# Stick-breaking attention ranked in front of the ten projection blocks of a hybrid mixer

## The chip, the core and the metric

The kernel runs on one core of a Trainium2 chip. The metric is the device time of one execution in microseconds, as the median of three runs. The profile is one further execution, recorded by the hardware profiler. Engines are named as the profile names them: PE is TensorE's matmul, PEld its weight load, DVE VectorE, ACT ScalarE, POOL GpSimd, SP the engine that issues most loads.

## The reference, cut to what matters

One transformer block on 512 tokens of width 1024, all in float32. The first half normalises the input, projects it, runs four mixers on the projections, gates and sums them:

```python
xn = _rms_norm(h, norm_mix_g)
(cb, cc, cx, uv, sb_q, sb_k, sb_v, fx_q, fx_k, fx_v, f_raw, gate_raw) = split(xn @ w_in)
y_a = _short_conv_mixer(cb, cc, cx, w_conv)                   # cb * conv3(cc * cx)
y_b = _spatial_gating_mixer(uv, w_s, b_s, ln_g, ln_b)         # gelu, layer norm of v, causal mix
y_c = _stick_breaking_attention(sb_q, sb_k, sb_v)             # 4 heads of 64
y_d = _forgetting_attention(rms(fx_q), rms(fx_k), fx_v, cumsum(log_sigmoid(f_raw + b_f)))
merged = sum_n sigmoid(gate_raw[n]) * (y_n @ w_branch[n])
h = h + merged @ w_out
h = h + _swiglu(_rms_norm(h, norm_ffn_g), w_ffn_in, w_ffn_out)
```

The change lies in the first half: the projections of `cc`, `cx`, `cb`, `fx_q`, `fx_k`, the gating mixer and the stick-breaking attention.

## The kernel before

Activations are kept transposed, 128 channels by 512 tokens to a tile. Every float32 product is made of three fp32r products of a high and a low part (`mm3`, L185 to L198): high by high, high by low, low by high. The weights' parts are made on the chip: `load_units` (L207) loads a chunk of 128x1024 on SP's queue into `raw`, then `split` (L179) copies it to `whi` on ACT (L180) and subtracts on DVE to get `wlo` (L181). `raw`, `whi` and `wlo` have three buffers each, and a tile's name carries a number that counts up in the order of the code (`whi_535` is the high part of the last chunk of the first token group).

The stretch around the change, in the order of the code:

- `u` blocks, then the first token group `wt1` (L377, four chunks, four PSUM banks of the pool "a", L196 to L198), which gives the gating mixer's v and the stick-breaking v; then gelu, layer norm and split of v into `vg` (L405 to L424), and the causal weights `wsh`, `wsl` (L428 to L434, with a load on ACT's queue and a select on POOL).
- `mixed(MIXED[:8])`, eight of the ten projection blocks. A block (`proj_block`) is 8 units of weights, that is one chunk, 24 matmuls of 512 columns into one of three PSUM banks "g". `conv_block` (L463) is for the convolution, `fox_block` (L441) for the forgetting q and k; the latter's norm is `fox_norm` (L451), two matmuls, a square root on ACT, a reciprocal on DVE.
- the gating mixer's 24 matmuls (L505 to L507), which read `vg`, in four banks "a" of the five.
- the second token group `wt2` (two chunks of 128x1040, four banks "a"), which gives the forgetting v and f.
- the four heads of the stick-breaking attention: `sb_scores` (L548, matmuls L567 to L569, absolute value on ACT L571), `sb_weights` (exp, log, splits, matmuls L600 to L609, exp), `values` (L530, L535). A head holds four banks "a" from its scores to its weights.
- `mixed(MIXED[8:])`, the last two blocks, then the forgetting attention, then four passes of gates: a gate block of 24 matmuls and a branch of 6 for each of eight d.

Within an engine the instructions are not issued in the order of the code. A scheduler takes the code's order as rank and, engine by engine, puts in the instruction of the lowest rank whose operands are ready on a timeline that it estimates; the result is one fixed order for each engine. So PE runs projection blocks and gates while a head of attention is on ACT and DVE. Each engine then runs its list in order, and an instruction that waits holds up all that stand behind it.

Of the kernel before, what the change touches and what calls it, by code (L numbers as in the profile page):

```python
# [51 lines left out]
MIXED = (("cc", 0), ("cx", 0), ("fxq", 0), ("cb", 0), ("fxk", 0), ("cc", 1), ("fxq", 1), ("cx", 1), ("fxk", 1), ("cb", 1))  # L52
# [75 lines left out]
def mixer_kernel(ctx, tc, xT, units, quads, wt1, wt2, wsT, small, out):  # L128
# [312 lines left out]
    def fox_block(n, b):  # L441
        t = slot("y")
        V.tensor_tensor(t, proj_block(OFF[n] + b * P), r1, op=ALU.mult)
        fx[n, b] = t
        sq = slot("tmp")
        S.activation(sq, t, AF.Square)
        sqh, sql = slot("tmp", F32R), slot("tmp", F32R)
        split(sqh, sql, sq)
        return n, t, sq, sqh, sql

    def fox_norm(n, t, sq, sqh, sql):  # L451
        ps = bank("g")
        PE.matmul(out=ps, lhsT=hm_r, rhs=sqh, start=True, stop=False)
        PE.matmul(out=ps, lhsT=hm_r, rhs=sql, start=False, stop=True)
        S.activation(sq, ps, AF.Sqrt, bias=eps)
        V.reciprocal(sq, sq)
        g = gq if n == "fxq" else sml[:, C_GK:C_GK + 1]
        V.scalar_tensor_tensor(t, t, g, sq, op0=ALU.mult, op1=ALU.mult)
# [4 lines left out]
    def conv_block(n, b):  # L463
        ps = proj_block(OFF[n] + b * P)
        if n == "cc":
            cv[b] = slot("gt")
            V.tensor_tensor(cv[b], ps, r1, op=ALU.mult)
        elif n == "cx":
            cx, acc = slot("gt"), slot("gt")
            V.tensor_tensor(cx, ps, r1, op=ALU.mult)  # L470
            V.tensor_tensor(cx, cv[b], cx, op=ALU.mult)
            w = [sml[:, C_CONV + 3 * b + i:C_CONV + 3 * b + i + 1] for i in range(3)]
            V.tensor_scalar(acc, cx, w[2], None, op0=ALU.mult)
            V.scalar_tensor_tensor(acc[:, 1:], cx[:, :T - 1], w[1], acc[:, 1:], op0=ALU.mult, op1=ALU.add)
            V.scalar_tensor_tensor(acc[:, 2:], cx[:, :T - 2], w[0], acc[:, 2:], op0=ALU.mult, op1=ALU.add)
            V.tensor_tensor(acc, acc, r1, op=ALU.mult)
            cv[b] = acc
        else:
            V.tensor_tensor(cv[b], ps, cv[b], op=ALU.mult)
            split(*y[0, b], cv[b])  # L480

    def mixed(blocks):
        norm = None
        for n, b in blocks:
            if n in ("fxq", "fxk"):
                norm = fox_block(n, b)
            else:
                conv_block(n, b)
                if norm:
                    fox_norm(*norm)  # L490
                norm = None

    mixed(MIXED[:8])


    for b in range(2):
        for c2 in range(2):
# [125 lines left out]
            scores = sb_scores(h + 1)  # L623
        values(h, sbv, *weights, [y[2, 0], y[2, 1]], js)

    mixed(MIXED[8:])


    before = sm.tile([P, NT, HEADS], F32, tag="before", bufs=1, name="before")
# [405 lines left out]
```

## Time and profile before

| what | us |
|---|---|
| median of 3 runs (792.93 to 793.89) | 793.47 |
| the profiled execution, whole | 792.95 |
| its span, first to last instruction | 791.2 |
| PE busy in the span | 785.9 |
| DVE busy | 546.5 |
| ACT busy | 367.8 |

The profiled execution takes 1.75 us more than its span. A matmul's busy time reaches past the start of the next one, since matmuls are pipelined; so PE's work is counted here from start to start, and a short wait shows as a longer step between two starts.

### The profile page before, as it was taken

The page shows a single profiled execution, that of the slowest core. Times are in us where ns is not written, and L with a number is a line of the kernel's source. Part 1 is how long each engine was busy: PE and PEld are TensorE (multiplying, and loading weights), DVE is VectorE, ACT ScalarE, POOL GpSimd, SP SyncE. Part 2 cuts the span into 40 slices and gives each one's busy share as a digit, 9 for nine tenths or more (in the row PEclk, how much of TensorE's full clock was granted, in tenths as well). Part 3 has the DMA queues.
Part 4 walks back from the last instruction along what each step waited for, and adds up shares of the span by engine and source line. Part 5 has one row for each costly group of instructions (what it writes and reads, how often), then busy time and mean ns, then how long its engine had stood idle before and what let it go on. Part 6 is the DMA issues. An engine that isn't in the chain of part 4 may idle for free.

```text
span 791.2 us, 10770 instructions
## 1 busy us (share of the span) xinstructions
PE 785.9 (99%) x4319; PEld 677.7 (86%) x4319; DVE 546.5 (69%) x780; ACT 367.8 (46%) x522; POOL 8.4 (1%) x23
## 2 busy tenths in 40 slices
PE   9999999999999999999999999999999999999998
PEld 6888888888888888888888888998899998899987
DVE  8447886877677688756665698873478874468752
ACT  7336427677743455434343554552155552135530
POOL 1000000000000000000000000000000000000000
PEclk9999999999999999999999999999999999999999
DMA  7423222222123222222243343352133333211021
GB/s 286 133 80 104 97 80 81 80 81 74 59 80 106 81 81 81 80 93 81 106 161 119 131 155 115 108 184 82 54 107 109 107 119 121 80 54 54 28 94 67
DMA packets 24098, 78.98 MB, mean 100 GB/s; under 512 B 2672, under 2 KB 2928, under 8 KB 24048
## 3 DMA queue, kind: packets, MB, share of 16 engines
q1 hardware_dynamic: 22608, 75.80, 28.4%
q10 hardware_dynamic: 1440, 2.49, 1.0%
q8 instruction: 34, 0.56, 0.3%
q14 instruction: 16, 0.13, 0.1%
HBM read 76.18 MB, written 2.10 MB: 99 GB/s over the span
## 4 chain that ended last, share of the span: by engine, by line
PE 97%; ACT 1%; DVE 0%; DMA 0%; issue 0%; SPq 0%
PE ps L187 65%; PE ps L891 8%; PE ps L892 8%; PE ps L890 7%; PE ps L198 1%; PE ps L196 1%; PE ps L197 1%; PE ps L535 1%; PE ps L701 1%; DMA raw<-units 0%; PE ps L685 0%; PE ps L601 0%; PE ps L568 0%; PE ps L600 0%; PE ps L686 0%; PE ps L569 0%
## 5 line engine op out<-in xcount | busy, mean ns | idle before, releaser
L187 PE MATMUL ps<-xg,whi 128*128 128x512 f32 (+1 forms) x1212 | 377.8, 393 | 0.5 <-DVE xg L181 0.3
L187 PEld LDWEIGHTS ps<-xg,whi 128*128 128x128 f32 x1212 | 226.2, 188 | 50.3 <-DVE xg L181 0.8
L187 PE MATMUL ps<-xg,wlo 128*128 128x512 f32 (+1 forms) x606 | 235.8, 393 | 0.0
L180 ACT ACTIVATE whi<-raw 128x1024 fp32r<-128x1024 f32 (+2 forms) x104 | 106.4, 1025 | 180.1 <-PE ps L187 135.7
L181 DVE TENSOR_TENSOR wlo<-raw,whi 128x1024 fp32r<-128x1024 f32 (+2 forms) x104 | 122.8, 1182 | 49.7 <-ACT whi L180 49.4
L891 PE MATMUL ps<-op,whi 128*128 128x256 f32 x504 | 141.0, 281 | 0.0
L890 PE MATMUL ps<-op,whi 128*128 128x256 f32 x504 | 140.6, 280 | 0.0
L892 PE MATMUL ps<-op,wlo 128*128 128x256 f32 x504 | 139.2, 281 | 0.0
L187 PEld LDWEIGHTS ps<-xg,wlo 128*128 128x128 f32 x606 | 113.9, 188 | 24.9
L180 ACT ACTIVATE whi<-sraw 128x1024 fp32r<-128x1024 f32 x63 | 66.9, 1062 | 97.3 <-PE ps L187 32.7
L890 PEld LDWEIGHTS ps<-op,whi 128*128 128x128 f32 x504 | 95.3, 189 | 0.2
L891 PEld LDWEIGHTS ps<-op,whi 128*128 128x128 f32 x504 | 94.7, 188 | 0.2
L892 PEld LDWEIGHTS ps<-op,wlo 128*128 128x128 f32 x504 | 93.9, 188 | 0.0
L181 DVE TENSOR_TENSOR wlo<-sraw,whi 128x1024 fp32r<-128x1024 f32 x63 | 77.1, 1224 | 23.1 <-ACT whi L180 22.9
L187 PE MATMUL ps<-y,whi 128*128 128x512 f32 x224 | 70.5, 394 | 0.0
L962 DVE TENSOR_TENSOR mrg<-ps,mrg 128x512 f32<-128x512 f32 (+1 forms) x25 | 16.7, 669 | 64.5 <-PE ps L187 64.5
L187 PEld LDWEIGHTS ps<-y,whi 128*128 128x128 f32 x224 | 42.0, 188 | 9.7
L187 PE MATMUL ps<-y,wlo 128*128 128x512 f32 x112 | 44.2, 394 | 0.0
L727 ACT ACTIVATE gt<-gt 128x512 f32<-128x512 f32 x32 | 20.1, 627 | 23.7 <-DVE gt L726 23.4
L726 DVE TENSOR_TENSOR gt<-ps,r 128x512 f32<-128x512 f32 x32 | 22.0, 687 | 11.3 <-PE ps L187 11.2
L187 PEld LDWEIGHTS ps<-y,wlo 128*128 128x128 f32 x112 | 21.0, 188 | 4.8
L737 DVE SCALAR_TENSOR_TENSOR gt<-gt,ps 128x512 f32<-128x512 f32 x24 | 16.4, 685 | 10.1 <-PE ps L187 6.7
(247 smaller groups left out, 827.7 us busy)
## 6 DMA issues: line engine op xcount, KB each, us to landing
raw<-units SPq DMA_DIRECT2D x90, 512.0 KB, 3.4
sraw<-quads SPq DMA_DIRECT2D x36, 512.0 KB, 4.5
x<-xT SPq DMA_DIRECT2D x8, 256.5 KB, 5.2
raw<-units SPq DMA_DIRECT2D x8, 256.0 KB, 5.2
raw<-wt SPq DMA_DIRECT2D x4, 512.0 KB, 3.9
tmp<-xT ACTq DMA_DIRECT2D x8, 256.0 KB, 3.6
outT<-mrg SPq DMA_DIRECT2D x7, 256.0 KB, 2.0
raw<-wt SPq DMA_DIRECT2D x2, 520.0 KB, 3.3
```

What stands on the lines that cost most here:

```text
L180: S.activation(dst_hi, src, AF.Copy)
L181: V.tensor_tensor(dst_lo, src, f(dst_hi), op=ALU.subtract)
L187: i = PE.matmul(**args)
L196: PE.matmul(out=ps, lhsT=ah, rhs=bh, start=start, stop=False)
L197: PE.matmul(out=ps, lhsT=al, rhs=bh, start=False, stop=False)
L726: V.tensor_tensor(t, proj_block(OFF["gate"] + n * D + d * P), r1, op=ALU.mult)
L727: S.activation(t, t, AF.Tanh, scale=0.5)
L737: V.scalar_tensor_tensor(t, t, 1.0, ps, op0=ALU.add, op1=ALU.mult)
L890: PE.matmul(out=dst, lhsT=wh[:, u], rhs=xh[:, k], start=first and k == 0 and jj == 0, stop=False, skip_group_check=True)
L891: PE.matmul(out=dst, lhsT=wh[:, u], rhs=xl[:, k], start=False, stop=False, skip_group_check=True)
L892: PE.matmul(out=dst, lhsT=wl[:, u], rhs=xh[:, k], start=False, stop=ends, skip_group_check=True)
L962: V.tensor_tensor(h1[d][:, cs], src, h1[d][:, cs], op=ALU.add)
```

## The change

The call of the first eight blocks is taken out of its place ahead of the gating mixer, and all ten blocks are called behind the stick-breaking attention. The order of the units in the weight stream is the same. Both programs have 4301 matmuls; the changed one has 20 loads of an activation table on ACT, the one before 16.

```diff
@@ -490,8 +490,6 @@
                     fox_norm(*norm)
                 norm = None
 
-    mixed(MIXED[:8])
-
 
     for b in range(2):
         for c2 in range(2):
@@ -623,7 +621,7 @@
             scores = sb_scores(h + 1)
         values(h, sbv, *weights, [y[2, 0], y[2, 1]], js)
 
-    mixed(MIXED[8:])
+    mixed(MIXED)
```

Line numbers behind L492 are two lower in the changed kernel (L505 becomes L503). The code now asks for the two chunks of `wt2` ahead of the first projection block, and for the attention's banks ahead of the blocks' work. Three places of the engines' lists follow.

PE at the end of the first token group. Before (`ps_628` and `ps_661` are the blocks cc 0 and cx 0):

```order
L187 MATMUL ps_628<-xg_310,whi_630 128x512 x2
L187 MATMUL ps_628<-xg_310,wlo_631 128x512
L187 MATMUL ps_661<-xg_139,whi_663 128x512 x2
L187 MATMUL ps_661<-xg_139,wlo_664 128x512
L187 MATMUL ps_661<-xg_163,whi_663 128x512 x2
```

Now (`ps_1161` and `ps_1194` are the same two blocks, `ps_628` to `ps_667` the gating mixer, `ps_684` the second token group):

```order
L187 MATMUL ps_1161<-xg_310,whi_1163 128x512 x2
L187 MATMUL ps_1161<-xg_310,wlo_1164 128x512
L187 MATMUL ps_1194<-xg_139,whi_1196 128x512 x2
L503 MATMUL ps_628<-big_622,vg 128x256
L503 MATMUL ps_641<-big_622,vg 128x256
L503 MATMUL ps_654<-big_622,vg 128x256
L503 MATMUL ps_667<-big_622,vg 128x256
L196 MATMUL ps_684<-whi_690,xg_139 128x260
```

The gating mixer, which stood behind four blocks (96 matmuls), now stands behind one block and two matmuls of the next.

ACT at the same place. Before:

```order
L180 ACTIVATE whi_535<-raw_533 128x1024
L180 ACTIVATE whi_630<-raw_629 128x1024
L180 ACTIVATE whi_663<-raw_662 128x1024
L396 ACTIVATE sbv_563<-ps_439,rc_337 128x4x64
L396 ACTIVATE sbv_563<-ps_440,rc_337 128x4x64
L413 ACTIVATE tmp_574,mu_575<-ps_439,rc_337 128x256
L396 ACTIVATE sbv_563<-ps_441,rc_337 128x4x64
L180 ACTIVATE whi_703<-raw_702 128x1024
```

Now, the first eight rows, and the seven that stand nine rows further on:

```order
L180 ACTIVATE whi_535<-raw_533 128x1024
L180 ACTIVATE whi_690<-raw_688 128x1040
L180 ACTIVATE whi_744<-raw_742 128x1040
L396 ACTIVATE sbv_563<-ps_439,rc_337 128x4x64
L396 ACTIVATE sbv_563<-ps_440,rc_337 128x4x64
L413 ACTIVATE tmp_574,mu_575<-ps_439,rc_337 128x256
L396 ACTIVATE sbv_563<-ps_441,rc_337 128x4x64
L180 ACTIVATE whi_1163<-raw_1162 128x1024
```

```order
L428 DMA tmp_618<-wsT 128x512
L419 ACT_TABLE_LOAD
L419 ACTIVATE var_573<-var_573,eps 128x4
L180 ACTIVATE whi_1196<-raw_1195 128x1024
L180 ACTIVATE big_622<-tmp_620 128x512
L180 ACTIVATE vg<-tmp_574 128x256 x2
L180 ACTIVATE vg<-tmp_587 128x256 x2
```

The two chunks of `wt2` (`whi_690`, `whi_744`) have taken the places of the first two projection chunks, and the first projection chunk stands where the third stood. In the built program `whi_535`, `whi_1163` and `whi_1196` have one and the same buffer; before, `whi_630`, `whi_663` and `whi_703` have three different ones.

ACT in the third head of the stick-breaking attention, from the exponential of its scores to the split of its sums. Before:

```order
L581 ACTIVATE big_1295<-big_1295 128x1280
L582 ACT_TABLE_LOAD
L582 ACTIVATE big_1295<-big_1295,one 128x1280
L539 ACTIVATE aug_1325<-ps_1316 64x512
L554 ACTIVATE aug_1373<-y_353 64x512
L555 ACTIVATE aug_1374<-y_349 64x512
L180 ACTIVATE whi_2313<-raw_2312 128x1024
L180 ACTIVATE big_1336<-big_1295 128x1280
```

Now, behind the exponential:

```order
L580 ACT_TABLE_LOAD
L580 ACTIVATE big_982<-big_982,one 128x1280
L455 ACT_TABLE_LOAD
L455 ACTIVATE tmp_1507<-ps_1547,eps 128x512
L180 ACTIVATE y_361<-gt_1461 128x512
L180 ACTIVATE whi_2098<-raw_2097 128x1024
L725 ACT_TABLE_LOAD
L725 ACTIVATE gt_1991<-gt_1991 128x512
L537 ACTIVATE aug_1012<-ps_1003 64x512
L552 ACTIVATE aug_1060<-y_353 64x512
L553 ACTIVATE aug_1061<-y_349 64x512
L180 ACTIVATE big_1023<-big_982 128x1280
```

The square root of a `fox_norm` and the tanh of a gate, each with a table load, now stand inside the head's chain.

## Rows read from the trace of the kernel before

**Rows 1.** Page: busy time of the engines; granted clock in 40 slices.

```profile
PE 785.9 (99%) x4319; PEld 677.7 (86%) x4319; DVE 546.5 (69%) x780; ACT 367.8 (46%) x522; POOL 8.4 (1%) x23
PEclk9999999999999999999999999999999999999999
```

**Rows 2.** Timeline, PE, end of first token group: start, us, engine, line, op, tiles.

```profile
62.15 0.39 PE L198 MATMUL ps<-wlo,xg 128*128 128x512 f32 x1
62.38 0.62 PE L187 MATMUL ps<-xg,whi 128*128 128x512 f32 x2
62.84 0.39 PE L187 MATMUL ps<-xg,wlo 128*128 128x512 f32 x1
...
109.59 0.28 PE L505 MATMUL ps<-big,vg 128*128 128x256 f32 x1
109.70 0.28 PE L506 MATMUL ps<-big,vg 128*128 128x256 f32 x1
```

**Rows 3.** Timeline, ACT and DVE: splits of weight chunks round that place.

```profile
56.78 1.06 ACT L180 ACTIVATE whi<-raw 128x1024 fp32r<-128x1024 f32 x1 [4.39 <-PE ps L197]
...
62.40 1.06 ACT L180 ACTIVATE whi<-raw 128x1024 fp32r<-128x1024 f32 x1
...
63.49 1.23 DVE L181 TENSOR_TENSOR wlo<-raw,whi 128x1024 fp32r<-128x1024 f32 x1 [0.41 <-ACT whi L180]
```

**Rows 4.** Timeline, PE and ACT: the one long wait of the stretch.

```profile
135.92 0.63 ACT L180 ACTIVATE tmp<-tmp 128x512 fp32r<-128x512 f32 x1
136.61 0.51 PE L453 MATMUL ps<-tmp,hm_r 128*128 128x512 f32 x1 [0.46 <-ACT tmp L180]
```

**Rows 5.** Timeline, ACT and DVE: the layer norm of v and its split.

```profile
67.95 1.06 ACT L180 ACTIVATE whi<-raw 128x1024 fp32r<-128x1024 f32 x1 [0.40 <-ACT tmp L417]
...
69.43 1.28 ACT L419 ACT_TABLE_LOAD   x1
70.72 0.30 ACT L419 ACTIVATE var<-var,eps 128x4 f32<-128x4 f32 x1
71.42 0.63 ACT L180 ACTIVATE big<-tmp 128x512 fp32r<-128x512 f32 x1 [0.40 <-POOL tmp L430]
73.31 0.75 ACT L180 ACTIVATE vg<-tmp 128x256 fp32r<-128x256 f32 x2 [1.26 <-DVE tmp L423]
...
72.86 0.75 DVE L423 TENSOR_TENSOR tmp<-tmp,sml 128x256 f32<-128x256 f32 x2
```

**Rows 6.** Timeline, ACT: a head's chain from its last scores.

```profile
180.87 0.28 ACT L571 ACTIVATE big<-ps 128x128 f32<-128x128 f32 x1 [0.79 <-PE ps L569]
181.18 1.27 ACT L581 ACTIVATE big<-big 128x1280 f32<-128x1280 f32 x1
182.47 1.28 ACT L582 ACT_TABLE_LOAD   x1
183.77 1.36 ACT L582 ACTIVATE big<-big,one 128x1280 f32<-128x1280 f32 x1
185.16 0.59 ACT L539 ACTIVATE aug<-ps 64x512 f32<-64x512 f32 x1
185.78 0.63 ACT L554 ACTIVATE aug<-y 64x512 fp32r<-64x512 f32 x1
...
186.95 1.06 ACT L180 ACTIVATE whi<-raw 128x1024 fp32r<-128x1024 f32 x1
187.91 1.26 ACT L180 ACTIVATE big<-big 128x1280 fp32r<-128x1280 f32 x1
```

**Rows 7.** Groups by line, ACT, 60 to 240 us: busy, mean ns | idle before.

```profile
L455 ACT ACTIVATE tmp<-ps,eps 128x512 f32<-128x512 f32 x4 | 2.8, 690 | 4.0 <-PE ps L454 4.0
```

**Rows 8.** Groups by line, DVE, 60 to 240 us: busy, mean ns | idle before.

```profile
L456 DVE RECIPROCAL tmp<-tmp 128x512 f32<-128x512 f32 x4 | 13.4, 3348 | 0.3 <-ACT tmp L455 0.3
L726 DVE TENSOR_TENSOR gt<-ps,r 128x512 f32<-128x512 f32 x12 | 8.2, 686 | 0.7 <-PE ps L187 0.7
L557 DVE CAST aug<-aug 64x512 fp32r<-64x512 f32 x2 | 0.8, 420 | 0.0
```

## The prediction, made before the changed kernel was run

> **What bounds the kernel now.** I read the page first. PE is busy 785.9 of 791.2 us, DVE 69%, ACT 46%, and the granted clock is full in all 40 slices, that is the 2.4 GHz level [rows 1]. Since both programs have the same 4301 matmuls, the time can only change by PE's waits. Busy time hides a short wait, so I then read PE's timeline from start to start: a matmul of 512 columns starts 0.23 us after the one before, one of 256 columns 0.11 to 0.12 us [rows 2], and smaller ones I take in proportion (an estimate from these). At the end of the first token group PE goes on without a gap: 62.15, 62.38, 62.84 [rows 2]. Two chunks are split ahead there: ACT makes a `whi` at 56.78 and one at 62.40, each started as soon as PE has left a buffer, and the latter is the third block's, not needed for another two blocks of 24 x 0.23 = 5.56 us [rows 3]. Between 60 and 240 us there is one long wait of PE: at 136.61 it stands 0.46 us idle, some 0.62 us over the usual step, for the high part of a square that `fox_norm` averages [rows 4]. So the change can win back 0.6 us in this stretch, and everything else that it does to PE is a loss or nothing.
>
> **The change part by part.** *Removed.* No instruction goes. The wait of 136.61 belonged to the ninth block's `fox_norm`; in the new list that norm stands behind a whole block of other work and its square is ready about 2 us ahead by sums as below. I book -0.6 us, between -0.6 and 0.
>
> *The first block behind the token group.* It needs `whi_1163`, and this has the buffer of `whi_535`, which the token group's last chunk is read from until about 62.3. ACT's list up to there is the old one, so the split runs 62.40 to 63.46, as it did for `whi_703` [rows 3]. PE would go on at 62.38 and starts at about 63.52 (0.06 us from ACT's end to PE's start, as 136.55 to 136.61 [rows 4]): 1.14 us. Two matmuls on the high part take 0.46, to 63.98; the third reads `wlo`, which DVE makes from 63.49 to 64.72 [rows 3], behind the same instructions as before: 0.79 us. Neither can be less, because there is no other buffer and nothing else in PE's list ahead of it.
>
> *The second block.* 22 x 0.2315 = 5.09 us later, at 69.86, PE wants `whi_1196`, which has the buffer of `whi_1163`. ACT can start when the last high matmul has read it, about 69.85, and takes 1.06: PE starts at 70.97, 1.11 us late. The cover that hid this split before was the third buffer; the chunks `whi_690` and `whi_744` of the second token group hold the other two, and their matmuls stand behind this block.
>
> *The gating mixer.* Two matmuls later, at 71.43, PE wants `vg`. Before, four blocks (22 us) hid the layer norm; now one block and these waits do. The variance's end moves from 71.02 to about 69.96, since the split of 67.95 to 69.01 is no longer in front of it; from there to the first `vg` are 2.29 us (71.02 to 73.31), and half of 0.75 for the first of the pair [rows 5]: 72.65. PE waits 1.25 us. `big_622` hangs on a load and POOL and is done at 72.05 as before, earlier than that [rows 5]. The second matmul wants `vg` of the other pair, for which DVE still has to do half of 0.75, a product of 0.69 with the projection and half of 0.75, then ACT its half: 1.25 us after the first, less the 0.12 of one matmul: 1.13 us. Since ACT now has `whi_1196` and `big_622` in front of `vg`, and the load is issued from ACT's queue behind the last square, these two may be 0.4 us longer each; they may be 0.3 shorter if the variance ends earlier. Sum of this stretch: 1.14 + 0.79 + 1.11 + 1.25 + 1.13 = 5.4 us, between 4.8 and 6.2. Behind it the 24 small matmuls, the second token group and the rest of the second block run on operands that are long made.
>
> *The attention.* Its heads now run beside the projection blocks, so that `fox_norm`'s square roots fall into the heads' chains, each with a table load. In the third head ACT's chain from the last scores to the split of the sums took 8.3 us (180.87 to 187.91 + 1.26) [rows 6]. The new list puts in a table load and square root (1.28 [rows 6] + 0.69 [rows 7]), one split of 512 columns (0.63 [rows 4]) and a table load and tanh (1.28 + 0.63): 4.5 us more, 12.8; with 0.28 from the last score matmul's start to ACT, 13.1. In that time PE's list gives 45 matmuls of 512 columns and 6 smaller: 45 x 0.2315 + 0.70 = 11.1. Taking 0.2 off for ACT's overlaps, PE waits 1.8 us, between 1 and 2.5. On DVE a reciprocal of 3.35 us [rows 8] waits for that square root and stands in front of the head's low parts: the next low part comes about 0.3 us late, and then the gate block whose bank waits for a product behind it, about 0.6. In the second head the same square root and reciprocal stand ahead of the square for the next `fox_norm`: 7.4 on ACT, 3.35, four DVE operations of about 0.69 and one of 0.42 [rows 8], two of 0.63 on ACT, 15.0 us against 14.3 of PE's 56 large and the smaller matmuls: 0.7 us, between 0 and 1.5. The first head has 11.6 us of PE against 9.0, the fourth has no square root in it: nothing. Sum 1.8 + 0.9 + 0.7 = 3.4 us, between 0 and 6.5.
>
> *What follows.* The attention ends some four gate pairs of 30 matmuls earlier in PE's list. In the trace of before nothing waits for its end, so this is worth nothing.
>
> **The sum.** 5.4 + 3.4 - 0.6 = 8.2 us. The profiled execution took 792.95 us whole, 1.75 over its span, so 801.2 by its own time; the median of the runs is 0.5 above it. I forecast 801.5.
>
> **The rivals.** *Only the first stretch costs (0.20).* If the attention's lists have more slack than my sums (the split done ahead of PE), 792.95 + 5.4 - 0.6 = 797.8. For it: over the span ACT is busy 46% only [rows 1]. Against: the chain of the third head is longer by rows, whatever the start.
>
> *DVE becomes the bound beside the attention (0.12).* A fox block brings DVE a split of 1.23, three operations of about 0.69 and a reciprocal of 3.35, 6.7 us in 5.56 us of PE, a gate pair about 2 x 0.69 + 1.25 x 1.23 = 2.9 in 6.95 [rows 2, 3, 8]. Four of them stand beside three heads now. If each head's second half slips by another 0.8 us, 804.5.
>
> *Not slower (0.04).* The two serial chunks do not bite: if the block's split ended by 62.38 and the next by 67.94, PE would go through as before, the layer norm would be met later in the list's own pace, and with the wait of 136.61 gone the time would be 792.3. It decides at the buffers: it holds if the three names do not share one, and they do.
>
> *A table load costs more than its row (0.02).* Six loads lie on the paths above: one ahead of the variance, two in the second head, three in the third. If ACT stood still ahead of each as long as the load itself takes, 6 x 1.28 = 7.7 us more: 809.2. Against it: the row of 182.47 starts 0.02 us after the end of the instruction before it, and the next one starts 0.02 after its own end [rows 6], so I count the load alone. The Trainium skill (ScalarE: Activation LUTs, "What ACT_TABLE_LOAD costs") adds a drain of about 1.38 us to a load of about 1.28. By that page the sum would be 8.3 us higher; the load agrees with the row, the drain the trace does not show.
>
> *The clock falls (0.02).* Five waits of about 1.1 us within 12 us thin PE's work. If the granted clock went to the 1.2 GHz level there, the 26 large and 3 small matmuls between the first and last wait, 6.4 us, would take twice as long (an estimate from the two levels): 807.9. Against it: the clock stayed full through the wait of 136.61 [rows 1, 4], though that is one wait and shorter. [...] The trace of before has no such group of waits.
>
> **How the numbers follow.** Forecast 0.60, the rivals 0.20, 0.12, 0.04, 0.02, 0.02. The range reaches from the first rival less the 0.6 by which its stretch may be shorter, 797.2, taken as 797.0, to the second and a little over, 805.0; "not slower", the table loads and the clock stay out. A measurement of this kernel tells about 0.2%, 1.6 us, from no change. Slower by more than that: all but the third rival and 0.02 of the first, 0.94; within it 0.05; faster 0.01, the rest of the third, as 0.6 us is all that I see to win.
>
> **What would show it.** In the profile of the changed kernel PE should stand idle five times between 62 and 75 us: for ACT `whi` (L180) and DVE `wlo` (L181) at about 62.4 and 64, for `whi` at 69.9, for `vg` at 71.4 and 72.8, and the gating mixer should come at about 73. In the third head PE should wait for ACT `big` (L180) ahead of L598 at some 165 us, and for `tmp` ahead of L453 at some 134. ACT should have 20 table loads. PE's start-to-start step should stay 0.23. The prediction is wrong if PE passes 62 to 75 us without those waits, if the waits there are longer because the load behind `big_622` is late, or if more of them appear from 100 to 200 us than two or three.

## The result

| what | before | changed |
|---|---|---|
| median, us | 793.28 (792.93 to 793.89, 4 runs) | 803.15 (802.66 to 803.34, 4 runs) |
| ratio to before | | 1.0123, 95% interval 1.0105 to 1.0140 |
| profiled execution, whole, us | 792.95 | 803.34 |
| its span, us | 791.2 | 801.6 |
| its mean granted clock | 1.000 | 0.998 |

The changed kernel is 9.9 us slower; forecast were 801.5 us, range 797 to 805. The page answers to [rows 1]:

```profile
PE 790.4 (99%) x4319; PEld 678.9 (85%) x4319; DVE 547.0 (68%) x780; ACT 373.5 (47%) x526; POOL 8.6 (1%) x23
PE   9997999999999999999999999999999999999998
PEclk9999999999999999999999999999999999999999
```

PE's share of busy time is still 99%, and both traces count 4319 instructions on PE, so no work was added. Only the fourth slice (60 to 80 us) shows that something is missing, and the clock's row shows nothing, since a slice is 20 us long. PE's timeline from 62 to 76 us answers to [rows 2] (start, duration, then in brackets the idle time before it and who ended it):

```profile
62.78 0.40 PE L198 MATMUL ps<-wlo,xg 128*128 128x512 f32 x1
64.14 0.72 PE L187 MATMUL ps<-xg,whi 128*128 128x512 f32 x2 [0.96 <-ACT whi L180]
65.40 0.50 PE L187 MATMUL ps<-xg,wlo 128*128 128x512 f32 x1 [0.54 <-DVE mu L414]
...
71.65 0.73 PE L187 MATMUL ps<-xg,whi 128*128 128x512 f32 x2 [0.91 <-ACT whi L180]
73.38 0.39 PE L503 MATMUL ps<-big,vg 128*128 128x256 f32 x1 [0.99 <-ACT vg L180]
74.65 1.01 PE L503 MATMUL ps<-big,vg 128*128 128x256 f32 x3 [0.88 <-ACT vg L180]
75.45 0.42 PE L196 MATMUL ps<-whi,xg 128*128 128x260 f32 x1
75.67 0.42 PE L197 MATMUL ps<-whi,xg 128*128 128x260 f32 x1
```

The five waits are there. Over the usual step they cost 1.13, 0.69, 1.08, 1.16 and 1.15 us, together 5.2. The last two rows show what was not in the sum: matmuls of 260 columns start 0.22 us apart, where the usual step is 0.12, as in the trace of before:

```profile
110.89 0.28 PE L196 MATMUL ps<-whi,xg 128*128 128x260 f32 x1
111.01 0.29 PE L197 MATMUL ps<-whi,xg 128*128 128x260 f32 x1
```

The view of busy time by stretch tells why. Each of its rows gives a stretch and its length, then busy time and count of PE, PEld, DVE, ACT and POOL, and behind POOL the granted clock as its share of full:

```profile
72.00:74.60 2.60, 0.77 (x3) 0.19 (x1) 2.60 (x8) 1.71 (x5) 0.00 (x0) 1.00 0.00 0
74.60:78.10 3.50, 3.45 (x16) 3.46 (x17) 2.96 (x6) 0.33 (x1) 0.00 (x0) 0.51 0.41 117
78.10:82.00 3.90, 3.90 (x34) 3.90 (x34) 1.68 (x4) 0.00 (x0) 0.00 (x0) 1.00 0.09 34
```

From the last wait on, for 3.4 us, the granted clock is at its lower level, 1.2 GHz. In the attention PE waits four times (timeline, PE):

```profile
138.36 0.50 PE L453 MATMUL ps<-tmp,hm_r 128*128 128x512 f32 x1 [0.31 <-ACT tmp L180]
...
169.07 0.91 PE L598 MATMUL ps<-big,ntri_r 128*128 128x128 f32 x4 [1.54 <-ACT big L180]
171.66 0.50 PE L599 MATMUL ps<-big,ntri_r 128*128 128x128 f32 x2 [0.17 <-DVE big L181]
...
172.92 0.73 PE L187 MATMUL ps<-xg,whi 128*128 128x512 f32 x2
```

Over the usual step these are 0.46, 1.71, 0.33 and 0.30, together 2.8 us. The wait of [rows 4] is gone. For a whole balance I added up, in each trace, by how much a start-to-start step of PE exceeds the mean step of its width in the kernel before (excesses under some 0.04 us are left out). The stretches are us of the span of the traced execution, whose time can differ from the median; the fill of e4 counts as work and not as excess; "before" has 1.0 in each of the last two from changes of shape, and in the first of them from its own wait.

| kernel | 0-62 | 62-83 | 83-115 | 115-155 | 155-240 | median, us |
|---|---|---|---|---|---|---|
| before | 0.3 | 0.0 | 0.0 | 1.0 | 1.1 | 793.28 |
| changed | 0.9 | 7.1 | 0.3 | 0.9 | 3.6 | 803.15 |
| e1 own buffers | 0.8 | 0.1 | 0.2 | 1.0 | 1.0 | 792.96 |
| e2 four in front | 0.8 | 0.0 | 0.3 | 0.4 | 0.9 | 792.67 |
| e3 behind the gating mixer | 0.4 | 0.0 | 10.5 | 1.0 | 1.0 | 803.65 |
| e4 fill of two waits | 1.1 | 3.7 | 0.3 | 0.9 | 3.7 | 802.07 |
| e5 no square root | 0.3 | 8.3 | 0.3 | 0.5 | 3.2 | 802.84 |
| e6 behind wt2 | 0.5 | 7.1 | 0.1 | 1.8 | 1.5 | 801.75 |
| e7 two in front | 0.3 | 1.5 | 0.2 | 4.4 | 2.6 | 799.86 |
| e9 neither | 0.5 | 5.6 | 0.3 | 0.5 | 1.1 | 798.89 |
| e10 e1 and e2 together | 0.1 | 0.0 | 0.2 | 2.5 | 1.0 | 794.18 |

So the two profiled executions differ by 7.1 us in the first stretch (5.2 of waits, 0.3 of the one long step right behind each of the first three, 1.6 of the slow clock), by 2.7 from 83 to 240 us, and by 0.6 ahead of 62 us. That last part lies in the first 8 us: the first product starts at 5.26 us against 5.13, and its first steps take 0.59, 0.43 and 0.27 us against 0.34, 0.23 and 0.24 in the trace of before. e5 and e7, whose code is the same there, have 0.3 as before, and e1, which is not slower, has 0.8: it varies from one execution to the next and is no part of the change.

### The profile page after: what moved, and what is told of

Its sections match the earlier page's. It is cut to its first block, busy times and chain, and to the rows that moved or that the text cites. A ratio compares the mean times of both kernels' runs of the same rounds, so it can differ in the third digit from the quotient of the medians.

```text
span 801.6 us, 10779 instructions
## 1 busy us (share of the span) xinstructions
PE 790.4 (99%) x4319; PEld 678.9 (85%) x4319; DVE 547.0 (68%) x780; ACT 373.5 (47%) x526; POOL 8.6 (1%) x23
## 4 chain that ended last, share of the span: by engine, by line
PE 94%; DVE 3%; ACT 2%; issue 1%
PE ps L187 62%; PE ps L889 7%; PE ps L890 7%; PE ps L888 7%; PE ps L196 1%; PE ps L197 1%; PE ps L198 1%; PE ps L533 1%; PE ps L699 1%; PE ps L239 1%; DVE tmp L456 0%; DVE wlo L181 0%; PE ps L683 0%; PE ps L566 0%; ACT L455 0%
## 5 line engine op out<-in xcount | busy, mean ns | idle before, releaser
L181 DVE TENSOR_TENSOR wlo<-raw,whi 128x1024 fp32r<-128x1024 f32 (+2 forms) x104 | 122.7, 1181 | 56.3 <-ACT whi L180 56.0
L181 DVE TENSOR_TENSOR wlo<-sraw,whi 128x1024 fp32r<-128x1024 f32 x63 | 77.0, 1223 | 23.6 <-ACT whi L180 23.6
L197 PE MATMUL ps<-whi,xg 128*128 128x512 f32 (+1 forms) x64 | 22.0, 346 | 0.0
```

The costliest lines, as they stand in the source:

```text
L181: V.tensor_tensor(dst_lo, src, f(dst_hi), op=ALU.subtract)
L197: PE.matmul(out=ps, lhsT=al, rhs=bh, start=False, stop=False)
```

## The experiments

**e1: the chunk gets other buffers.** In `token_group`:

```diff
+            if wt is wt2 and c == 0:
+                hi, lo = big(F32R)[:, :nk * width], big(F32R)[:, :nk * width]
+            else:
                 ...                          # hi and lo from wpool, as before
```

> The changed kernel, but the high and low part of the first chunk of the second token group get two of the four large buffers that the gating weights and the heads use, so that the first projection block no longer has the chunk buffer of the first token group. If the five waits between 62 and 75 us come from the shared buffer, a second and a third block now stand in PE's list ahead of the gating mixer, all five waits are gone, the granted clock stays at 2.4 GHz, and of the change only what the attention costs is left (2.9 us in the changed kernel's trace, less the 0.6 won): 793.3 + 2.3 = 795.6 us, between 792.7 and 796.5. If the layer norm's chain or the early split of the second token group's chunks costs the time, whatever the buffers, the waits add up to the same 5 us and the time is 801 to 803 us.

Measured: 792.96 us, ratio 0.9995 (0.9986 to 1.0005). The view by stretch shows PE without a gap and the clock full:

```profile
60.00:80.00 20.00, 20.00 (x91) 16.29 (x90) 15.01 (x33) 13.04 (x32) 0.63 (x1) 1.00 0.38 120
80.00:120.00 40.00, 40.00 (x240) 35.52 (x239) 32.31 (x59) 22.97 (x32) 0.00 (x0) 1.00 0.23 77
120.00:160.00 40.00, 40.00 (x189) 32.69 (x188) 37.91 (x54) 31.18 (x44) 1.04 (x2) 1.00 0.21 69
160.00:200.00 40.00, 40.00 (x193) 33.34 (x192) 30.13 (x49) 30.04 (x39) 0.99 (x2) 1.00 0.24 79
```

The five waits hang on the shared buffer: with it gone the list has nearly three blocks (66 matmuls) ahead of the gating mixer and they cover the layer norm. But the attention's waits went too, which I had not expected, although the ten blocks still rank behind the heads.

**e2: four blocks in front.**

```diff
+    mixed(MIXED[:4])
...
-    mixed(MIXED)
+    mixed(MIXED[4:])
```

> The changed kernel with the first four of the ten blocks called ahead of the gating mixer again, the other six behind the attention. If the cost has two separate parts, the first stretch is as in the kernel before (no wait from 62 to 110 us), and the attention with four square roots beside it still costs between 1 and 3 us: 795.0 us, between 793.5 and 796.5. If the attention's waits were only a consequence of the first stretch, 792.7 to 793.3. If the attention costs by itself as much as the whole, 800 us or more.

Measured: 792.67 us, ratio 0.9991 (0.9981 to 1.0001). My expectation of 795 missed in the same way: no wait in the attention, although six blocks stand beside it. So either that cost follows from the first stretch, or from where exactly the norms fall. e5, e9 and e10 take this up.

**e3: past the gating mixer alone.** The kernel before, with `mixed(MIXED[:8])` moved from ahead of the gating mixer to between it and the second token group.

> The kernel before with the first eight blocks called behind the gating mixer, but still ahead of the second token group; the last two stay behind the attention. If what costs is that the blocks pass the second token group, whose chunks then take their buffers, PE still finds blocks to run until the gating mixer's operands are made: 793.3 us, between 792.5 and 794.0, with no wait of 1 us between 60 and 110 us. If passing the gating mixer is what uncovers the layer norm, PE waits 2.3 us or more for it: 795.6 to 799 us.

Measured: 803.65 us, ratio 1.0130 (1.0114 to 1.0145), outside both expectations. There is no wait for `vg`. PE has one long wait, 7.8 us, at another place, and a short one of 0.58 us idle at 147 us (timelines, DVE and PE; `mx` and `mrg` belong to the gating mixer, L443 is the product that opens a forgetting block):

```profile
82.07 0.43 DVE L512 TENSOR_TENSOR mx<-ps,sml 64x256 f32<-64x256 f32 x1
...
91.71 0.42 DVE L513 TENSOR_TENSOR mrg<-mx,mrg 64x256 f32<-64x256 f32 x1
92.83 0.69 DVE L181 TENSOR_TENSOR y<-mrg,y 128x512 fp32r<-128x512 f32 x1 [0.69 <-ACT y L180]
93.53 0.69 DVE L443 TENSOR_TENSOR y<-ps,r 128x512 f32<-128x512 f32 x1
```

```profile
87.42 0.39 PE L187 MATMUL ps<-xg,wlo 128*128 128x512 f32 x1
95.60 0.80 PE L453 MATMUL ps<-tmp,hm_r 128*128 128x512 f32 x1 [7.80 <-ACT tmp L180]
```

The forgetting block's last matmul starts at 81.87, but its product on DVE only at 93.53: fourteen operations of 0.42 us for the gating mixer, with splits and one product between them, now stand ahead of it. PE's list has `fox_norm` behind the next block alone, which ends at 87.65, and its operand is made 8 us later. The rank of the blocks against the gating mixer does matter, by DVE's order and not by the layer norm. In the changed kernel PE has 72 matmuls of the second token group and the first head's scores between the gating mixer and that block's end, its product starts 0.4 us after its last matmul does, and this wait does not appear.

**e4: throwaway matmuls in the last two waits.** The changed kernel with, ahead of the matmuls of each of the gating mixer's first two banks:

```diff
+            if b == 0:
+                w = (wsh[:, 0], vh[:, 0, 0:P])[c2]
+                for _ in range(5):
+                    PE.matmul(out=ps, lhsT=w, rhs=xh[0], start=True, stop=True)
```

> The changed kernel with ten throwaway matmuls of 512 columns (five on the gating weights ahead of the first matmul of the gating mixer, five on the first vg ahead of the second); their sums are overwritten. They stand in the last two of the five waits and should be hidden there, PE's list being the same otherwise. If those waits are what lets the clock fall to 1.2 GHz at 74.7 us, the granted clock stays full and the time is the 1.6 us lower that the slow stretch costs: 803.15 - 1.6 = 801.5 us, between 800.9 and 802.2. If the first three waits suffice for it, the clock falls as before and the time stays 803.2, or rises by up to 0.5 us for fill that isn't hidden.

Measured: 802.07 us, ratio 1.0109 (1.0094 to 1.0124). Timeline, PE:

```profile
72.79 1.44 PE L500 MATMUL ps<-xg,big 128*128 128x512 f32 x5 [0.20 <-ACT big L180]
74.07 0.28 PE L507 MATMUL ps<-big,vg 128*128 128x256 f32 x1
74.19 1.32 PE L500 MATMUL ps<-xg,vg 128*128 128x512 f32 x5
75.34 0.52 PE L507 MATMUL ps<-big,vg 128*128 128x256 f32 x3
75.70 0.28 PE L196 MATMUL ps<-whi,xg 128*128 128x260 f32 x1
75.81 0.28 PE L197 MATMUL ps<-whi,xg 128*128 128x260 f32 x1
```

The step of 260 columns is 0.12 again and all four runs have a mean granted clock of 1.000. The fill overshoots: the second `vg` matmul starts at 75.34, not at 74.65 plus the 0.21 that this trace lags already at 64 us, so 0.48 us late. 803.15 - 802.07 + 0.48 = 1.6 us is what the slow clock cost, as expected; only that the fill would be hidden whole was wrong. In these four executions the three earlier waits, still open, did not lower the clock by themselves; in e9 below the first two did.

**e8 and e11: one of the two waits filled** (`c2 == 1` alone, `c2 == 0` alone).

> The changed kernel with only the five throwaway matmuls on the first vg, which fill the last of the five waits; four waits stay open. If the last wait is the one that lets the clock fall, it stays full through 62 to 82 us. If the whole group of waits does it, the clock falls again at about 74 to 75 us, for about as long, and the matmuls of the second token group then take 0.217 us each as in the changed kernel. The lists behind the second token group differ from the changed kernel's, so only this stretch is compared.

> The changed kernel with only the five throwaway matmuls on the gating weights, which fill the fourth of the five waits; the last, some 0.7 us of it, stays open. Filling the last one alone kept the clock full. If any one of the two does, it stays full here too; if it is the last wait before the second token group that counts, the granted clock falls to half again at about 74 us. Only this stretch is compared.

The clock stayed full from 62 to 82 us in both, so in these two executions filling either was enough. Their lists are planned anew further on, and the one run of each (800.26 and 804.85 us) is not compared. In e11 PE waits 2.5 us once more in the attention, 2.30 of it idle, and there the clock falls too (granted clock 0.57 from 171 to 175 us), with no other wait in the 8 us ahead of it.

**e5: the square root's table load taken out of the heads.** The changed kernel:

```diff
-        S.activation(sq, ps, AF.Sqrt, bias=eps)
+        S.activation(sq, ps, AF.Copy)
```

> The changed kernel with the square root of the forgetting norm (L455) replaced by a copy without the added epsilon, so q and k are normed wrongly; the lists of PE and DVE are the same, on ACT the four copies stand where the square roots stood, and five table loads are gone. If the third head waits because the square root's table load stands in ACT's chain and costs what its row shows, the wait ahead of L598 shrinks by 1.28 us from 1.71 to 0.4, the one ahead of L453 in the second head (0.46) goes, and those for the next low part and the gate bank (0.33 and 0.30) stay, since DVE's reciprocal moves with ACT: 803.15 - 1.8 = 801.4 us, between 800.9 and 801.8. If a load costs twice its row, all four waits go: 800.2 us. If the reciprocal on DVE is what sets the chain, the wait ahead of L598 stays above 1.2 us: 802.4 to 803.2.

Measured: 802.84 us (801.66 to 803.07), ratio 1.0117 (1.0101 to 1.0132). The time lies in the range of the third expectation, but its sign, a wait above 1.2 us ahead of L598, did not appear, so none of the three holds. In the traced execution the clock stayed at the lower level for 6.8 us (granted clock 0.50 from 74 to 80 us), which hides part of the gain: the two runs with a mean granted clock of 0.995 took 803.07 and 803.03 us, the two with 0.998, as in the changed kernel, 801.66 and 802.65. In the attention itself the wait ahead of L453 went, under 0.1 us, and the one ahead of L598 fell to 0.19, below the 0.4 expected, but the one for the low part grew from 0.33 to 1.20 (timelines, DVE, then PE, of e5):

```profile
160.69 1.68 DVE L584 SCALAR_TENSOR_TENSOR big<-ps,big 128x512 f32<-128x512 f32 x4 [1.00 <-ACT big L580]
162.29 3.34 DVE L456 RECIPROCAL tmp<-tmp 128x512 f32<-128x512 f32 x1
...
169.83 1.49 DVE L181 TENSOR_TENSOR big<-big,big 128x1280 fp32r<-128x1280 f32 x1
```

```profile
167.69 0.91 PE L598 MATMUL ps<-big,ntri_r 128*128 128x128 f32 x4
171.38 0.50 PE L599 MATMUL ps<-big,ntri_r 128*128 128x128 f32 x2 [0.96 <-DVE big L181]
```

The rows of the changed kernel beside them (DVE, ACT):

```profile
162.56 3.35 DVE L456 RECIPROCAL tmp<-tmp 128x512 f32<-128x512 f32 x1 [0.32 <-ACT tmp L455]
167.75 1.27 ACT L180 ACTIVATE big<-big 128x1280 fp32r<-128x1280 f32 x1
```

The reciprocal starts at 162.56 there and at 162.29 here: it stands behind the head's four sums (L584), which do not get earlier, so it did not follow the square root. ACT's table loads and DVE's reciprocal bound the head almost alike, and to take the load away is worth 0.8 us of the 2.8 (0.4 each from 115 to 155 and from 155 to 240 us). The reciprocal alone was not taken out.

**e9: neither square root nor reciprocal.** As e5, and `V.reciprocal(sq, sq)` becomes `V.tensor_tensor(sq, sq, sq, op=ALU.mult)`.

> The changed kernel with the forgetting norm's square root replaced by a copy and its reciprocal by a product of 0.7 us, so q and k are normed wrongly; four table loads and four reciprocals of 3.35 us are gone, and the lists behind the first stretch are planned anew. If the heads wait because such a square root and, behind it, such a reciprocal stand in their chain on ACT and DVE, the attention's 2.9 us go and the first stretch's 7 us stay: 803.15 - 2.9 = 800.3 us, between 799.7 and 801.3. If the heads are late for another reason (the blocks' splits and products beside them), the waits stay: 802.4 to 803.2.

Measured: 798.89 us (797.94 to 800.21), ratio 1.0070 (1.0056 to 1.0084). No wait of PE is left in the attention (0.5 and 1.1 us in the table), which fits that the 2.8 us hang on the norm's work in the heads; since the lists behind the first stretch were planned anew, it does not prove it. The traced execution took 798.13 us, 2.3 less than the 800.4 that 803.34 and the attention's 2.9 would leave, and 1.5 of that lie in the first stretch: the clock fell earlier, behind the first two waits, and was back at 69.3 (timeline, PE):

```profile
66.19 1.06 PE L187 MATMUL ps<-xg,whi 128*128 128x512 f32 x2
...
73.69 0.38 PE L503 MATMUL ps<-big,vg 128*128 128x256 f32 x1
74.30 0.62 PE L503 MATMUL ps<-big,vg 128*128 128x256 f32 x3 [0.23 <-ACT vg L180]
```

The slow matmuls ran while the layer norm was on ACT and DVE, so the waits for `vg` shrank from 1.16 and 1.15 to 0.26 and 0.50. The four times lie in two pairs, 797.94 and 798.13, 799.66 and 800.21; where the clock fell in those without a trace isn't known.

**e6: the heads rank behind eight blocks again.** `mixed(MIXED[:8])` between the second token group and the attention.

> The changed kernel with the first eight blocks called between the second token group and the attention, so that they rank in front of the heads again; the lists of PE, ACT and DVE up to the gating mixer are those of the changed kernel. If the first stretch costs 5.2 us of waits and 1.7 of the slow clock by itself, and the attention's 2.9 us come only from square roots that stand in the third head, which they don't here: 793.2 - 0.6 + 6.9 = 799.5 us, between 799 and 801. If the ranks of the heads don't matter for those waits, 802 to 803.2.

Measured: 801.75 us (799.96 to 802.21), ratio 1.0101 (1.0084 to 1.0118). The first stretch is 7.1 us for the 6.9 expected. But 799.5 was expected in all and the rival named 802 or more, and the measured time lies between: the attention was cheaper than in the changed kernel (3.3 us from 115 to 240 us against 4.5) and not free: PE waits 0.23, 0.88 and 0.42 us at 132, 143 and 157 us, the last one for a bank that a norm's square root has yet to read.

**e7: two blocks in front.** `mixed(MIXED[:2])` ahead of the gating mixer.

> The changed kernel with the first two of the ten blocks ahead of the gating mixer. Two blocks are 48 x 0.23 = 11.1 us of matmuls behind 62.4 us, so PE meets the first vg at 73.5 us, when it is just made (72.9 + 0.4), and has parts of a third block between the matmuls of the gating mixer. If the shared buffers and the uncovered layer norm are the whole cost, nearly all of it goes with two blocks: 793.6 us, between 792.5 and 794.8, clock full. If the second token group's chunks still take the third block's buffers, PE stands 1 to 3 us at the third block: 795 to 797.

Measured: 799.86 us, ratio 1.0082 (1.0067 to 1.0097); expected were 793.6. The first stretch does nearly as expected (1.5 us of small waits are left). The miss is in the attention (timelines, PE and ACT):

```profile
152.36 0.33 PE L567 MATMUL ps<-mask_sb,ident_r 128*128 128x128 f32 x1 [2.05 <-ACT big L612]
...
154.36 0.77 PE L187 MATMUL ps<-y,whi 128*128 128x512 f32 x2 [1.26 <-ACT tmp L455]
```

```profile
149.66 1.06 ACT L180 ACTIVATE whi<-raw 128x1024 fp32r<-128x1024 f32 x1 [5.23 <-PE ps L187]
150.74 1.28 ACT L612 ACT_TABLE_LOAD   x1
152.03 0.28 ACT L612 ACTIVATE big<-ps 128x128 f32<-128x128 f32 x1
152.33 1.28 ACT L455 ACT_TABLE_LOAD   x1
153.62 0.69 ACT L455 ACTIVATE tmp<-ps,eps 128x512 f32<-128x512 f32 x1
```

ACT idles 5.2 us because a chunk's split stands first in its list and waits for PE; behind it queue the exponential that frees a head's bank and the square root that frees a norm's bank, each with a table load, and PE waits for both banks. The clock falls there too. The runs with a mean granted clock of 0.997 and 0.998 took 799.11 and 799.28 us, the two with 0.995 took 800.52 and 800.44.

**e10: e1 and e2 together**, which puts the last norm into the second head's chain.

> Both edits that took the time away, together: four blocks ahead of the gating mixer, and two of the large buffers for the first chunk of the second token group. The first stretch has nothing to wait for. In the lists the last forgetting norm now stands in the second head's chain: its table load and square root between the logarithm and the split on ACT, its reciprocal right ahead of the low part on DVE. If that place is what makes the heads late, PE waits 0.5 to 2 us in the second head and the time is 793.8 us, between 793.2 and 795. If the attention's waits came with the first stretch only, it is 792.7 us.

Measured: 794.18 us, ratio 1.0010 (1.0001 to 1.0019), as expected from the norm's place. Timelines, PE and ACT:

```profile
149.94 0.73 PE L187 MATMUL ps<-xg,whi 128*128 128x512 f32 x2 [1.21 <-ACT tmp L458]
```

```profile
145.58 1.37 ACT L585 ACTIVATE big<-big,one 128x1280 f32<-128x1280 f32 x1
...
147.91 1.28 ACT L458 ACT_TABLE_LOAD   x1
149.20 0.69 ACT L458 ACTIVATE tmp<-ps,eps 128x512 f32<-128x512 f32 x1
149.79 1.26 ACT L180 ACTIVATE big<-big 128x1280 fp32r<-128x1280 f32 x1
```

The square root stands between the head's logarithm and its split, reads its bank late, and PE's next block waits 1.4 us for that bank. Nothing waits in the first stretch here, so such a wait needs no loss ahead of it. In e1 and e2 no norm's reciprocal begins within a head's chain (from the exponential to L598) in the second to fourth head; in the changed kernel two do, at 130.7 and 162.6 us.

**e12: e2 in more rounds.**

> The kernel with four blocks in front, in more rounds, to tell whether it beats the kernel before. Its trace lacks the wait of 0.6 us that the kernel before has at 136.61 us and has no other in its place: 792.7 us, ratio 0.9993. If that wait's time comes back elsewhere, the ratio is 1.000.

Measured: 792.35 us (792.07 to 792.86, 11 runs), ratio 0.9987 (0.9978 to 0.9996). With four blocks in front and six behind the attention the kernel beats the kernel before by 1.2 us (793.51 beside it), where about 0.6 was expected. Its trace has no wait at 136 us and none in its place, which accounts for 0.6; the other half has no cause on record, and the medians of one kernel differ by 0.3 from one set of runs to another (this one 792.67 and 792.35).

## Why the prediction was right, point by point

- *First block, second block, gating mixer (1.14, 0.79, 1.11, 1.25, 1.13).* Measured 1.13, 0.69, 1.08, 1.16, 1.15: 5.2 for 5.4. e1 shows the cause, the chunk buffer, by taking it away. The trace names `mu` (L414) as the releaser of the second wait; but the matmul reads the low part, which DVE had made at 65.35, 0.05 us ahead of its start, and in e6 the same wait is put down to `wlo` (L181).
- *Third head (1.8).* Measured 1.71. But the ground of the attention's terms was only half right: e5 shows DVE's reciprocal to be as much a bound as ACT's loads, so that the chain on ACT alone did not set the price of the norm.
- *Low part 0.3, gate bank 0.6, second head 0.7.* Measured 0.33, 0.30 and 0.46. The last lies within its bounds of 0 to 1.5, the other two had none; the gate bank's term was twice too large. The parts given for the second head add up to 15.2 us and not 15.0, so its term should have been 0.9, twice what came.
- *The wait of 136.61 (-0.6).* It went, as booked.
- *The clock.* Here the forecast failed: the rival "the clock falls", given 0.02, came true. The step that failed is the one that spoke against it: that the clock stayed full through one wait of 0.46 us [rows 1, 4] says nothing of five waits of 0.5 to 1.0 us in 12 us. Its price was off the other way, 6.4 us for a measured 1.6: I let the clock be low from the first wait to the last, over 26 large matmuls, and it fell at the last one, for 3.4 us, with 15 matmuls of 256 and 260 columns. The Trainium skill (TensorE: Matmul & The Clock Gate, "HAM oscillation — how this bites in real kernels") speaks of gaps longer than any of these five; by that section the clock would have stayed up here, and the measurement decides.
- *The table loads.* The rival of a double price did not occur: with a load out of ACT's list in e5 the split (167.75 in the changed kernel, 166.36 in e5) comes 1.5 us sooner behind the head's last score (156.25 and 156.39), which is the load's own 1.28 and the copy's being 0.12 shorter than the root, and no second 1.28.
- *The sum.* 792.95 + 5.2 + 2.8 - 0.6 = 800.4 from the terms as measured, 1.6 for the clock, 0.3 for the long steps behind waits, 0.6 for the start, 0.4 for small steps: 803.3, the profiled 803.34. The forecast for that execution was 801.15, 2.2 short: the clock and the long steps (1.9) and the start and small steps (1.0) were missing, and its other terms were 0.8 too high. So the mechanism of the waits was right, and that the number came within 1.65 us of the median in spite of the clock is in part luck, since errors of opposite sign met.

What stays open: why the clock falls at the last wait in three traced executions with this first stretch (the changed kernel, e5, e6) and behind the second in that of e9; the runs tell only that it stayed up in the six executions with one or both of the last two waits filled. How ACT and DVE share the price of the attention's 2.8 us is shown for the table load alone (e5): the lists of e6 to e9 were planned anew, so what they tell of the attention is of their lists.

## What to carry to other kernels

When work is ranked back, look at what inherits its buffers: here not the blocks' own work but the early splits of another group's chunks took the buffers that had covered a layer norm, and a pair of idle large buffers gave all of it back. A dense kernel's short waits can cost more than their length once several lie close together, because the clock may fall behind them; read the granted clock by stretches of a few us, since a page's slice of 20 us hides it. A long operation with a table load (here a norm's square root and reciprocal) is free beside an attention head and cost 0.5 to 2.3 us inside its chain here, and which of the two a new order brings must be read from the order of each engine.

## What the runs showed of the hardware that was not expected

- Five waits, none with more than 1.04 us idle, brought TensorE's granted clock to 1.2 GHz for 3.4 us (in the traced execution of e5 6.8); the matmuls of 260 columns took 0.217 us a step instead of 0.119, which cost 1.6 us. In e9 the first two of them, 0.96 and 0.54 us idle, did so alone; two waits of 2.05 and 1.26 us idle close together (e7) did so too. A single wait of 2.30 us idle (e11) did, and one of 7.8 us (e3), whose stretch lost some 2.5 us more than the wait itself (10.5 less 7.95). Single waits of 1.54 us (the third head of the changed kernel) and 1.21 us (e10) did not.
- Slow matmuls are not always lost time: where the next operand was late anyway (e9), the same 3.4 us at the lower level were largely paid out of the waits behind them.
- A reciprocal of 128x512 takes 3.35 us on DVE, more than a table load and the square root together (1.28 and 0.69), and is thereby the second bound that appears when the load is removed.
